# Feed-forward in four groups of inner tiles, with all but three or four tile pairs by Strassen's algorithm

## The chip, the cores and the metric

The kernel runs on one core of one Trainium2 chip. Times are device microseconds of one execution. The trace is that of one profiled execution; its engines are TensorE (PE, with its weight loads as PEld), VectorE (DVE), ScalarE (ACT), GpSimd (POOL) and SyncE (SP), which issues the DMAs.

## The reference

The program is a trunk of two layers on 512 tokens of 1024 features, all in float32. Each layer has a feed-forward, a mixer and a second feed-forward:

```python
for layer in range(DEPTH):
    x = x + 0.5 * swiglu(rmsnorm(x, ffa_norm[layer]), ffa_gate[layer], ffa_up[layer], ffa_down[layer])
    ...                                  # the mixers, which the change leaves alone
    x = x + mix
    x = x + 0.5 * swiglu(rmsnorm(x, ffb_norm[layer]), ffb_gate[layer], ffb_up[layer], ffb_down[layer])
return rmsnorm(x, final_norm)

def swiglu(x, wg, wu, wd):
    return (jax.nn.silu(x @ wg) * (x @ wu)) @ wd
```

The inner width is 2816, so a feed-forward has three products of 512 x 1024 x 2816.

## The kernel before

**Layout.** Features lie on the 128 partitions and tokens along the free dimension: `x` is 8 tiles of 128 x 512. The inner width is 22 tiles of 128 (`NF`), worked on in two halves of 11 (`HF`).

**A split product.** Each float32 operand is kept as two fp32r parts, high and low, and a product is three matmuls, high x high, high x low and low x high (`mm3`, lines 246 to 248). The two parts of a weight are made on the core: a DMA brings a raw piece of 128 x up to 1024 (`wraw`, three buffers), ScalarE copies it to the high part (line 274) and VectorE subtracts to get the low one (line 275; three buffers of each).

**A plain pair** ("S" in `PLAN`) is one inner tile of gate and up: 2 x 8 contraction tiles x 3 matmuls of 512 columns. VectorE then multiplies both with the row scale `rstd`, ScalarE takes Silu of the gate, VectorE multiplies the two and the result is split again (`hhi`, `hlo`; 11 buffers each).

**A Strassen pair** ("W", `hidden7`) does the same tile as a 2 x 2 block product: gate and up, two halves of the tokens, even and odd contraction tiles. It is 7 products of 4 contraction tiles x 3 matmuls of 256 columns (line 490). VectorE first makes the four weight sums (lines 467 and 468) and their low parts (line 474), ScalarE the high ones (line 473); afterwards ScalarE and VectorE join the results (lines 495 to 508). The sums on the side of `x` are the **column forms** (`column_forms`, lines 440 to 450): for each pair of contraction tiles four sums of 128 x 256 and their two parts, kept in the four `xi` buffers for the whole feed-forward. They are made right before the first Strassen pair. Their two inputs are scaled copies of `x` in the pool `t`, which has three buffers and serves the squares and the root mean square as well.

**The down projection** follows each half: for each pair of output tiles, 11 inner tiles x 2 x 3 matmuls of 512 columns, then VectorE adds half of the result to `x` (line 415). In the second half `set_x` makes the high and low part of the new `x`, its squares and their sum; after the last tile `set_rstd` sums them over the partitions with a matmul of ones (line 320), takes Sqrt on ScalarE and a reciprocal on VectorE (line 324).

**Order.** Every engine runs its instructions in the order that a scheduler wrote when the program was built; the program's own order sets the priorities. All raw pieces come by SP's queue, in order.

Of the kernel before, what the change touches and what calls it, by code (L numbers as in the profile page):

```python
# [12 lines left out]
AF = mybir.ActivationFunctionType  # L13
ALU = mybir.AluOpType
AX = mybir.AxisListType

P = 128
T = 512
NT = T // P
D = 1024  # L20
KD = D // P
DFF = 2816
NF = DFF // P
HF = NF // 2
# [89 lines left out]
          ("head", 2), ("val", 3), ("head", 3), ("outc", 0), ("outm", 0)]  # L114
OUT_LAST = ORDER1[-1][0]

PLAN = ("SSWSWSWWSWS", "SWSWWSWSWWS")
SCALE_DVE = ((1, 1), (3, 1))


class Trunk:
# [194 lines left out]
    def set_rstd(self, place=-70):  # L316
        nc = self.nc
        p = self.psum("aux")
        with self.tc.high_priority(place):
            nc.tensor.matmul(p, self.ones, self.acc, start=True, stop=True)  # L320
        s = self.temp()
        self.act(s, p, AF.Sqrt, bias=self.eps, scale=1.0 / D)
        self.rstd = self.cp.tile([P, T], F32, name="rstd")
        nc.vector.reciprocal(self.rstd, s)

    def load_x(self, norm, first=()):

# [39 lines left out]

    def ffn(self, wg, wu, wd, norm, load=None, out=None):
        nc = self.nc
        norm_in, self.forms = load or self.norm_in, None  # L370
        with self.phase("ffn", TURNS if load is None else TURNS[:-1]):
            if load is not None:
                self.load_x(load, (wg, wu))
            for half in range(2):
                hs = []
                for i in range(HF):
                    ft = half * HF + i
                    if PLAN[half][i] == "W":
                        if self.forms is None:
                            self.forms = self.column_forms(norm_in)  # L380
                        hs.append(self.hidden7(wg, wu, ft))
                        continue
                    ws = [self.ready.pop(0) if self.ready else self.column_weights(w, ft * P) for w in (wg, wu)]
                    pg, pu = self.psum(), self.psum()
                    cut = KD - 1 if ft == 0 else KD
                    for k0, k1 in ((0, cut), (cut, KD)):
                        for p, w in zip((pg, pu), ws):
                            for k in range(k0, k1):
                                self.mm3(p, (w[0][:, k], w[1][:, k]), self.xw[k], k == 0, k == KD - 1)
                    if self.rstd is None:  # L390
                        self.after_load()
                    g = self.tile("g")
                    nc.vector.tensor_mul(g, pg, self.rstd)
                    self.act(g, g, AF.Silu)
                    u = self.tile("u")
                    nc.vector.tensor_mul(u, pu, self.rstd)
                    nc.vector.tensor_mul(u, u, g)
                    hs.append(self.split_hidden(u))
                for dp in range(0, KD, 2):
                    if out is not None and half and dp == KD - 2:  # L400
                        self.last_down(wd, dp, hs, out)
                        continue
                    pd = [self.psum(), self.psum()]
                    for i0 in range(0, HF, 4):
                        n = min(4, HF - i0)
                        r0 = (half * HF + i0) * P
                        w = self.weights([(0, wd[r0:r0 + n * P, dp * P:dp * P + 256].rearrange(
                            "(k p) c -> p k c", p=P))], (n, 256))
                        for j, p in enumerate(pd):
                            for i in range(n):  # L410
                                self.mm3(p, (w[0][:, i, j * P:j * P + P], w[1][:, i, j * P:j * P + P]), hs[i0 + i],
                                         i0 + i == 0, i0 + i == HF - 1)
                    for j, p in enumerate(pd):
                        x = self.x[dp + j]
                        nc.vector.scalar_tensor_tensor(x, p, 0.5, x, op0=ALU.mult, op1=ALU.add)
                        if half:
                            self.set_x(dp + j, x, norm)
                            if out is not None:
                                self.finish_part(dp + j, range(NT))

    def split_hidden(self, u):
        hi, lo = self.tile("hhi", dt=FR), self.tile("hlo", dt=FR)
# [92 lines left out]
    def last_down(self, wd, dp, hs, out):  # L515

        nc = self.nc
        ws = []
        for i0 in range(0, HF, 4):
            n = min(4, HF - i0)  # L520
            r0 = (HF + i0) * P
            ws.append(self.weights([(0, wd[r0:r0 + n * P, dp * P:dp * P + 256].rearrange("(k p) c -> p k c", p=P))], (n, 256)))
        for th in range(2):
            cols, tiles = slice(256 * th, 256 * th + 256), range(2 * th, 2 * th + 2)
            pd = [self.psum()[:, :256] for _ in range(2)]
            for i in range(HF):
                w, h = ws[i // 4], [t[:, cols] for t in hs[i]]
                for j, p in enumerate(pd):
                    self.mm3(p, (w[0][:, i % 4, j * P:j * P + P], w[1][:, i % 4, j * P:j * P + P]), h, i == 0, i == HF - 1)
            for j, p in enumerate(pd):  # L530
                x = self.x[dp + j][:, cols]
                nc.vector.scalar_tensor_tensor(x, p, 0.5, x, op0=ALU.mult, op1=ALU.add)
                sq = self.temp()[:, :256]
                nc.scalar.activation(sq, x, AF.Square)
                nc.vector.tensor_add(self.acc[:, cols], self.acc[:, cols], sq)
                self.finish_part(dp + j, tiles)
            self.finish(out, tiles)
# [929 lines left out]
```

## Time and profile before

| | us |
|---|---|
| runs shown, median of 3 | 2189.73 (2188.24 to 2191.12) |
| the profiled execution, its own time | 2189.41 |
| its span, from the first to the last instruction | 2187.6 |
| TensorE busy | 2142.3 (98%) |
| VectorE busy | 1470.8 (67%) |
| ScalarE busy | 988.4 (45%) |

Matmuls are pipelined, so the durations of single ones overlap; the distance from start to start is what counts. The four feed-forwards are about 14.8 to 382.6, 776.5 to 1135.3, 1135.3 to 1495.3 and 1815.5 to 2178.2 us of the span; the mixers lie between.

### The profile page before, as it was taken

Reading aid. Unit: us, or ns where it says so; the run is one execution under the profiler, and the core shown is the slowest. Engines: PE = TensorE matmul, PEld = TensorE weight load, DVE = VectorE, ACT = ScalarE, POOL = GpSimd, SP = SyncE. Lnnn points to the kernel's source line nnn. Section 1 sums busy time; section 2 is a strip of 40 time slices with the busy share of each in tenths; the row PEclk is TensorE's granted clock in tenths of the full one; section 3 lists DMA queues with packets and bytes.
Section 4 is the critical chain, followed back from the end, with each engine's and each line's share of the span. In section 5 each row is a group of like instructions: output and inputs, shape, how many; then the busy total and the mean of one; then the engine's idle time right before and its main releaser. Section 6 shows DMA issues by size and latency. Waiting matters only on the chain.

```text
span 2187.6 us, 32169 instructions
## 1 busy us (share of the span) xinstructions
PE 2142.3 (98%) x12942; PEld 1766.3 (81%) x12942; DVE 1470.8 (67%) x2418; ACT 988.4 (45%) x1689; POOL 69.5 (3%) x70
## 2 busy tenths in 40 slices
PE   7999999999999999999999999999999999999998
PEld 5888998776667679889888989987777767988987
DVE  6854764787778788457549737745787767945753
ACT  6532443534434465234436424433368845523433
POOL 1000001000000020000010000001000001000000
PEclk9999999999999999999999999999999999999999
DMA  4433333311111034233333333326421122323331
GB/s 121 116 95 98 103 95 113 94 49 52 42 51 38 30 87 116 89 111 100 94 90 87 114 92 104 103 90 158 116 63 34 31 63 73 111 93 110 97 99 66
DMA packets 304805, 190.74 MB, mean 87 GB/s; under 512 B 19446, under 2 KB 299792, under 8 KB 304656
## 3 DMA queue, kind: packets, MB, share of 16 engines
q1 hardware_dynamic: 303536, 187.58, 29.5%
q8 instruction: 101, 1.65, 0.3%
q0 software_dynamic: 1120, 1.11, 0.3%
q14 instruction: 48, 0.39, 0.1%
HBM read 181.32 MB, written 2.10 MB: 84 GB/s over the span
## 4 chain that ended last, share of the span: by engine, by line
PE 92%; DVE 5%; ACT 1%; DMA 1%; issue 1%; POOL 0%; SPq 0%; ACTq 0%; DVEq 0%; POOLq 0%
PE ps L246 20%; PE ps L247 20%; PE ps L248 20%; PE ps L490 19%; PE ps L826 1%; PE ps L1356 1%; PE ps L808 1%; PE ps L1353 1%; DVE wlo L275 1%; DVE xi L450 1%; PE ps L1159 1%; PE ps L1337 1%; PE ps L1206 1%; PE ps L1012 0%; PE ps L929 0%
## 5 line engine op out<-in xcount | busy, mean ns | idle before, releaser
L275 DVE TENSOR_TENSOR wlo<-wraw,whi 128x1024 fp32r<-128x1024 f32 (+2 forms) x337 | 383.2, 1138 | 297.5 <-ACT whi L274 296.6
L274 ACT ACTIVATE whi<-wraw 128x1024 fp32r<-128x1024 f32 (+2 forms) x337 | 329.5, 981 | 561.8 <-PE ps L247 429.3
L246 PE MATMUL ps<-xhi,whi 128*128 128x512 f32 x1096 | 441.3, 403 | 1.0 <-ACT x L345 0.7
L247 PE MATMUL ps<-xlo,whi 128*128 128x512 f32 x1096 | 440.4, 402 | 0.4 <-DVE xlo L293 0.4
L248 PE MATMUL ps<-xhi,wlo 128*128 128x512 f32 x1096 | 439.5, 401 | 0.6
L247 PE MATMUL ps<-hlo,whi 128*128 128x512 f32 (+1 forms) x726 | 278.1, 383 | 0.0
L248 PE MATMUL ps<-hhi,wlo 128*128 128x512 f32 (+1 forms) x726 | 278.0, 383 | 0.0
L246 PE MATMUL ps<-hhi,whi 128*128 128x512 f32 (+1 forms) x726 | 277.8, 383 | 0.0
L247 PEld LDWEIGHTS ps<-xlo,whi 128*128 128x128 f32 x1096 | 208.5, 190 | 46.6 <-issue 6.1
L246 PEld LDWEIGHTS ps<-xhi,whi 128*128 128x128 f32 x1096 | 208.7, 190 | 46.1 <-issue 2.9
L248 PEld LDWEIGHTS ps<-xhi,wlo 128*128 128x128 f32 x1096 | 208.2, 190 | 45.3 <-DVE wlo L275 2.7
L490 PE MATMUL ps<-xi,shi 128*128 128x256 f32 x1056 | 193.9, 283 | 1.7 <-ACT shi L473 1.7
L490 PEld LDWEIGHTS ps<-xi,shi 128*128 128x128 f32 x1056 | 164.3, 192 | 2.6 <-ACT shi L473 1.9
L246 PEld LDWEIGHTS ps<-hhi,whi 128*128 128x128 f32 x726 | 136.5, 188 | 26.7
L247 PEld LDWEIGHTS ps<-hlo,whi 128*128 128x128 f32 x726 | 136.5, 188 | 26.5
L248 PEld LDWEIGHTS ps<-hhi,wlo 128*128 128x128 f32 x726 | 136.4, 188 | 26.4
L490 PE MATMUL ps<-xi,slo 128*128 128x256 f32 x528 | 148.4, 283 | 0.4 <-DVE slo L474 0.4
L474 DVE TENSOR_TENSOR slo<-sum,shi 128x1024 fp32r<-128x1024 f32 x88 | 107.5, 1221 | 24.0 <-ACT shi L473 24.0
L473 ACT ACTIVATE shi<-sum 128x1024 fp32r<-128x1024 f32 x88 | 93.1, 1059 | 63.5 <-DVE sum L468 30.2
L314 POOL TENSOR_TENSOR t<-t 128x512 f32<-128x512 f32 x35 | 53.0, 1514 | 1641.0 <-ACT t L310 1254.4
L490 PEld LDWEIGHTS ps<-xi,slo 128*128 128x128 f32 x528 | 100.8, 192 | 1.2 <-DVE slo L474 0.8
L490 PE MATMUL ps<-xhi,wlo 128*128 128x256 f32 x352 | 99.6, 283 | 0.0
(421 smaller groups left out, 3551.6 us busy)
## 6 DMA issues: line engine op xcount, KB each, us to landing
wraw<-in_ffa_gate_dram SPq DMA_DIRECT2D x44, 512.0 KB, 3.8
wraw<-in_ffa_up_dram SPq DMA_DIRECT2D x44, 512.0 KB, 3.8
wraw<-in_ffb_gate_dram SPq DMA_DIRECT2D x44, 512.0 KB, 3.8
wraw<-in_ffb_up_dram SPq DMA_DIRECT2D x44, 512.0 KB, 3.9
wraw<-in_ffa_down_dram SPq DMA_DIRECT2D x32, 512.0 KB, 3.4
wraw<-in_ffb_down_dram SPq DMA_DIRECT2D x32, 512.0 KB, 3.4
wraw<-in_ab_w_in_dram SPq DMA_DIRECT2D x26, 512.0 KB, 3.9
wraw<-in_cd_w_in_dram SPq DMA_DIRECT2D x18, 512.0 KB, 3.9
```

What stands on the lines that cost most here:

```text
L246: mm(out, w[0], x[0], start=start, stop=False)
L247: mm(out, w[0], x[1], start=False, stop=False)
L248: mm(out, w[1], x[0], start=False, stop=stop)
L274: nc.scalar.activation(h, raw, AF.Copy)
L275: nc.vector.tensor_sub(l, raw, h.bitcast(F32))
L314: (nc.gpsimd if self.norm_next and self.rstd is not None else nc.vector).tensor_add(self.acc, self.acc, sq)
L450: nc.vector.tensor_sub(lo, t, hi.bitcast(F32))
L473: nc.scalar.activation(hi, t, AF.Copy)
L474: nc.vector.tensor_sub(lo, t, hi.bitcast(F32))
L490: nc.tensor.matmul(out, a[:, j], b, start=first and i + j == 0, stop=i + j == 5, skip_group_check=True)
L808: mm(p[:, c * P:(c + 1) * P], BK[h, 4 * q + c, :], AR[h, 4 * q + c, :], start=True, stop=True)
L826: mm(p[h, c * LC:(c + 1) * LC], lhs[h, c, :], rhs[h, c, :], start=True, stop=True)
```

## The change

The inner tiles are taken in four groups of 5, 6, 5 and 6 instead of two halves of 11. After each pair of a group, one down part of the group before is done, as long as there is one (four parts: two output tiles each, with that group's tiles only); the last group's four parts come at the end. Only the first 4 pairs of the first feed-forward and the first 3 of the others are plain. The column forms are made behind the matmuls of the plain pair 2 (first feed-forward) or 0 (the others). The root mean square is taken as exp(-0.5 ln(mean + eps)) on ScalarE. `last_down`, the last part of the last feed-forward, takes 6 inner tiles instead of 11. Weight pieces of the down projection have up to 3 inner tiles instead of 4.

```diff
-PLAN = ("SSWSWSWWSWS", "SWSWWSWSWWS")
+PLAN = (("SSSSW", "WWWWWW", "WWWWW", "WWWWWW"), ("SSSWW", "WWWWWW", "WWWWW", "WWWWWW"))
...
-        self.act(s, p, AF.Sqrt, bias=self.eps, scale=1.0 / D)
+        self.log_exp_table()
+        self.act(s, p, AF.Ln, bias=self.eps, scale=1.0 / D)
         self.rstd = self.cp.tile([P, T], F32, name="rstd")
-        nc.vector.reciprocal(self.rstd, s)
+        self.act(self.rstd, s, AF.Exp, scale=-0.5)
...
+            below, ft = [], 0
+            for group in plan:
                 hs = []
+                for i, form in enumerate(group):
+                    hs.append((ft, self.hidden7(wg, wu, ft) if form == "W" else self.hidden8(wg, wu, ft, norm_in, plan)))
+                    ft += 1
+                    if below:
+                        self.down(wd, *below.pop(0))
+                below = [(dp, hs) for dp in range(0, KD, 2)]
+            for dp, hs in below:
+                if out is not None and dp == KD - 2:
+                    self.last_down(wd, dp, hs, out)
+                    continue
+                self.down(wd, dp, hs)
+                for k in (dp, dp + 1):
+                    self.set_x(k, self.x[k], norm)
+                    if out is not None:
+                        self.finish_part(k, range(NT))
+
+    def hidden8(self, wg, wu, ft, norm, plan):
...
+        if self.rstd is None:
+            self.after_load()
+        if ft == plan[0].index("W") - 3 + (plan is PLAN[0]):
+            self.forms = self.column_forms(norm)
+        g = self.tile("g")
+        nc.vector.tensor_mul(g, pg, self.rstd)
...
+    def down_weights(self, wd, dp, hs):
+
+        parts = [hs[i:i + 3] for i in range(0, len(hs), 3)]
+        return [(*self.weights([(0, wd[part[0][0] * P:(part[-1][0] + 1) * P, dp * P:dp * P + 256].rearrange(
+            "(k p) c -> p k c", p=P))], (len(part), 256)), [h for _, h in part]) for part in parts]
+
+    def down_products(self, out, j, part, cols, first, last):
+        hi, lo, hs = part
+        for i, h in enumerate(hs):
+            self.mm3(out, (hi[:, i, j * P:j * P + P], lo[:, i, j * P:j * P + P]), [t[:, cols] for t in h],
+                     first and i == 0, last and i == len(hs) - 1)
+
+    def down(self, wd, dp, hs):
+        pd = [self.psum(), self.psum()]
+        parts = self.down_weights(wd, dp, hs)
+        for part in parts:
+            for j, p in enumerate(pd):
+                self.down_products(p, j, part, slice(0, T), part is parts[0], part is parts[-1])
+        for j, p in enumerate(pd):
+            x = self.x[dp + j]
+            self.nc.vector.scalar_tensor_tensor(x, p, 0.5, x, op0=ALU.mult, op1=ALU.add)
```

## Rows read from the trace of the kernel before

**Rows 1.** The page's busy time of each engine, with share and instructions.

```profile
PE 2142.3 (98%) x12942; PEld 1766.3 (81%) x12942; DVE 1470.8 (67%) x2418; ACT 988.4 (45%) x1689; POOL 69.5 (3%) x70
```

**Rows 2.** The chain that ended last, by engine and by line.

```profile
PE 92%; DVE 5%; ACT 1%; DMA 1%; issue 1%; POOL 0%; SPq 0%; ACTq 0%; DVEq 0%; POOLq 0%
PE ps L246 20%; PE ps L247 20%; PE ps L248 20%; PE ps L490 19%; PE ps L826 1%; PE ps L1356 1%; PE ps L808 1%; PE ps L1353 1%; DVE wlo L275 1%; DVE xi L450 1%; PE ps L1159 1%; PE ps L1337 1%; PE ps L1206 1%; PE ps L1012 0%; PE ps L929 0%
```

**Rows 3.** Windows: one Strassen pair, one plain, two Strassen, one half's down projection.

```profile
core 0: us, PE busy (x) PEld busy (x) DVE busy (x) ACT busy (x) POOL busy (x), PEclk, DMA share, GB/s
971.41:981.48 10.07, 10.07 (x86) 10.07 (x84) 8.11 (x11) 6.07 (x9) 0.00 (x0) 1.00 0.36 104
981.48:992.39 10.91, 10.91 (x51) 9.02 (x49) 9.66 (x16) 3.48 (x5) 0.00 (x0) 1.00 0.28 82
992.39:1012.54 20.15, 20.15 (x170) 20.15 (x168) 16.42 (x24) 12.23 (x19) 0.00 (x0) 1.00 0.39 114
900.69:960.53 59.84, 59.84 (x266) 49.55 (x264) 21.77 (x25) 12.51 (x13) 0.00 (x0) 1.00 0.30 91
```

**Rows 4.** Windows: two Strassen and two plain pairs from each feed-forward's first Strassen pair.

```profile
38.98:93.23 54.25, 46.02 (x265) 40.46 (x264) 51.73 (x81) 31.92 (x44) 0.00 (x0) 0.91 0.34 98
799.98:848.65 48.67, 45.69 (x266) 40.24 (x264) 43.54 (x66) 26.44 (x38) 0.00 (x0) 0.93 0.36 98
1158.03:1205.94 47.91, 44.54 (x266) 39.14 (x264) 43.21 (x66) 26.65 (x38) 0.00 (x0) 0.96 0.35 99
1838.23:1886.63 48.40, 45.42 (x266) 40.12 (x265) 43.43 (x66) 26.39 (x39) 0.00 (x0) 0.93 0.36 99
```

**Rows 5.** Timeline of TensorE in the second feed-forward's first Strassen pair: start, length.

```profile
803.45 0.40 PE L247 MATMUL ps<-xlo,whi 128*128 128x512 f32 x1
805.69 0.39 PE L490 MATMUL ps<-xi,whi 128*128 128x256 f32 x1 [1.85 <-ACT xi L449]
...
808.80 0.63 PE L246 MATMUL ps<-xhi,whi 128*128 128x512 f32 x1
809.23 0.63 PE L247 MATMUL ps<-xlo,whi 128*128 128x512 f32 x1
```

**Rows 6.** Timeline of VectorE, five instructions in a row with no idle time.

```profile
1014.14 0.41 DVE L508 TENSOR_TENSOR u<-u,ps 128x256 f32<-128x256 f32 x1
1014.47 0.69 DVE L509 TENSOR_TENSOR g<-g,rstd 128x512 f32<-128x512 f32 x1
1015.07 0.68 DVE L511 SCALAR_TENSOR_TENSOR u<-u,rstd 128x512 f32<-128x512 f32 x1
1015.67 1.22 DVE L474 TENSOR_TENSOR slo<-sum,shi 128x1024 fp32r<-128x1024 f32 x1
1016.81 0.69 DVE L512 TENSOR_TENSOR u<-u,g 128x512 f32<-128x512 f32 x1
```

**Rows 7.** Timeline of the second feed-forward's root mean square and column forms.

```profile
788.19 1.02 PE L320 MATMUL ps<-t,c_main 128*128 128x512 f32 x2
788.57 2.36 DVE L275 TENSOR_TENSOR wlo<-wraw,whi 128x1024 fp32r<-128x1024 f32 x2 [4.36 <-ACT whi L274]
...
790.80 0.69 ACT L182 ACTIVATE t<-ps,eps 128x512 f32<-128x512 f32 x1
791.38 1.32 ACT L440 ACTIVATE t<-x,vecs_mix 128x512 f32<-128x512 f32 x2
791.52 3.35 DVE L324 RECIPROCAL rstd<-t 128x512 f32<-128x512 f32 x1 [0.59 <-ACT t L182]
...
812.36 1.23 DVE L450 TENSOR_TENSOR xi<-sum,xi 128x1024 fp32r<-128x1024 f32 x1 [0.52 <-ACT xi L449]
```

**Rows 8.** Timeline: a Strassen pair's last matmul and the end of its hidden tile.

```profile
1064.46 0.28 PE L490 MATMUL ps<-xi,slo 128*128 128x256 f32 x1
...
1068.09 0.69 DVE L424 TENSOR_TENSOR hlo<-u,hhi 128x512 fp32r<-128x512 f32 x1 [0.70 <-ACT hhi L423]
```

**Rows 9.** The page's DMA issues: KB of one, median us to landing.

```profile
wraw<-in_ffb_gate_dram SPq DMA_DIRECT2D x44, 512.0 KB, 3.8
```

More of the change, by code (lines that the diff above doesn't have):

```diff
@@ L369, in ffn @@
         nc = self.nc
-        norm_in, self.forms = load or self.norm_in, None
+        norm_in, plan = load or self.norm_in, PLAN[load is None]
         with self.phase("ffn", TURNS if load is None else TURNS[:-1]):
@@ L373, in ffn @@
                 self.load_x(load, (wg, wu))
-            for half in range(2):
+            below, ft = [], 0
+            for group in plan:
                 hs = []
[L376 to L419, printed above, removed]
@@ new lines, in hidden8 @@
+    def hidden8(self, wg, wu, ft, norm, plan):
+        nc = self.nc
+        ws = [self.ready.pop(0) if self.ready else self.column_weights(w, ft * P) for w in (wg, wu)]
+        pg, pu = self.psum(), self.psum()
+        cut = KD - 1 if ft == 0 else KD
+        for k0, k1 in ((0, cut), (cut, KD)):
+            for p, w in zip((pg, pu), ws):
+                for k in range(k0, k1):
+                    self.mm3(p, (w[0][:, k], w[1][:, k]), self.xw[k], k == 0, k == KD - 1)
+        if self.rstd is None:
[4 more added lines that the diff above has]
+        nc.vector.tensor_mul(g, pg, self.rstd)
+        self.act(g, g, AF.Silu)
+        u = self.tile("u")
+        nc.vector.tensor_mul(u, pu, self.rstd)
+        nc.vector.tensor_mul(u, u, g)
+        return self.split_hidden(u)
@@ L517, in last_down @@
         nc = self.nc
[L518 to L522, printed above, removed]
+        parts = self.down_weights(wd, dp, hs)
         for th in range(2):
@@ L525, in last_down @@
             pd = [self.psum()[:, :256] for _ in range(2)]
-            for i in range(HF):
-                w, h = ws[i // 4], [t[:, cols] for t in hs[i]]
+            for part in parts:
                 for j, p in enumerate(pd):
-                    self.mm3(p, (w[0][:, i % 4, j * P:j * P + P], w[1][:, i % 4, j * P:j * P + P]), h, i == 0, i == HF - 1)
+                    self.down_products(p, j, part, cols, part is parts[0], part is parts[-1])
             for j, p in enumerate(pd):
```

## The prediction

> **What bounds the kernel now.** I read the page first: TensorE is busy for 98% of the span, VectorE for 67% [rows 1], and the chain that ended last is TensorE's for 92%, with the three matmuls of a split product at 20% each and the line of Strassen's products at 19% [rows 2]. So a microsecond taken from TensorE's stream in a feed-forward is one taken from the end, as long as the other engines keep it fed. Next I read the windows of single pieces of one feed-forward [rows 3]: a Strassen pair is 10.07 us for 84 matmuls of 256 columns (0.1199 us each), a plain pair 10.91 us for 48 of 512 columns (0.2273 each), a half's down projection 59.84 us for 264 (0.2267 each). In all three TensorE has no gap and the clock is full. Last I read the four places where a feed-forward makes its first Strassen pair [rows 4]: each window holds two pairs of either kind, so 2 x 10.07 + 2 x 10.91 = 41.96 us of matmuls, and takes 54.25, 48.67, 47.91 and 48.40 us. There TensorE's mean clock is 0.91 to 0.96. The timeline shows why [rows 5]: TensorE waits for the column forms (lines 449 and 450), and after the wait a 512-column matmul starts every 0.43 us instead of every 0.227, that is at 1.2 GHz in place of 2.4.
>
> **The change, part by part.**
>
> *Pairs.* Before, 44 of 88 pairs are Strassen's. After, the first feed-forward keeps 4 plain ones and the others 3: 13 plain, 75 Strassen. 31 pairs go from 10.91 to 10.07 us: 31 x 0.84 = 26.0 us less. The interval is a little more than half for half the columns, so each matmul has a fixed part and the saving is 7.7% of a pair, not an eighth. The Trainium skill ("TensorE: Matmul & The Clock Gate", Back-to-back issue gap) gives N / 2.4 GHz + 2.5 ns, by which a pair would save 1.19 us and the sum would be 36.9 us. The rows do not agree with so small a fixed part, and the rows decide.
>
> *Column forms.* They move from just before the first Strassen pair to behind the matmuls of pair 0 (pair 2 in the first feed-forward), and there are now three (four) plain pairs ahead of the first Strassen pair instead of two. Today the four windows lose 199.23 - 4 x 41.96 = 31.4 us [rows 4]. If the forms are there in time all of that comes back. They cannot start much sooner than now: they need two of the three buffers of the pool t, of which the sum of squares holds one until the ones matmul at 788.19, and today they start at 791.38 and the last is written at 812.36 [rows 7]. But the need moves: the third product, the first that reads a form, starts 2.9 us (24 matmuls) into a pair that begins about 11 us later, near 814.
>
> *Root mean square.* Sqrt and a VectorE reciprocal of 3.35 us [rows 7] become Ln and Exp on ScalarE, each about the 0.69 us of the Sqrt row. It frees 3.3 us of VectorE, six times, and the scale is ready some 2.7 us sooner. TensorE works on other pairs or projections meanwhile, so I count 0 (bounds: 0, and 5 x 2.7 = 13 us if every start hung on it). One table load stays one table load.
>
> *Down parts.* The products are the same 528 x 512 columns a feed-forward. A part is 6 matmuls a tile: 6.80 us for 5 tiles, 8.16 for 6. Added are 16 additions into x a feed-forward (VectorE, 0.60 us each by the starts in [rows 6]) and 8 weight pieces with their DMA, copy and subtraction. They run under TensorE; without that cover they would cost 16 x 0.60 + 8 x about 0.6 = 14 us a feed-forward. Traffic: a pair and a part of 5 tiles bring 1.70 MB in 16.9 us, 101 GB/s, under the 114 GB/s of the stretch with two Strassen pairs [rows 3]; a piece lands in 3.8 us [rows 9]. SP issues pieces in order into three buffers, so a late VectorE subtraction delays the next piece; nothing else stands behind it. In the last part the half-width matmuls fall from 132 to 72: 0.4 us less.
>
> *VectorE's load.* By starts, an instruction of 256 columns holds it 0.33 us, of 512 0.60, of 1024 1.14 [rows 6]. A Strassen pair has four of the first, nine of the second and three of the third: 1.32 + 5.40 + 3.42 = 10.15 us, as much as its 10.07 on TensorE. A plain pair is 2 x 1.14 + 4 x 0.60 = 4.68, a part of 5 tiles about 0.85 + 0.60 + 2 x 0.60 = 2.65 (768 columns put between 512 and 1024). So in the second group VectorE has 6 x 10.15 + 4 x 2.65 = 71.5 us for TensorE's 6 x 10.07 + 4 x 6.80 = 87.6: 82%. Only a run of Strassen pairs with no part between them has no slack. There are four such runs a feed-forward, of two or three pairs. The stretch of two today shows no gap on TensorE [rows 3].
>
> *New stalls.* (a) From 788.6 until a first form is needed near 814 VectorE must do the weights of two plain pairs (2.36 + 2.28), four forms (each 4 x 0.33 + 1.14 = 2.46, in all 9.8), two plain pairs' ends (4 x 1.2 = 4.8) and of the Strassen pair one weight, two sums and one split (1.14 + 1.2 + 1.14): 22.7 of 25.4 us, and the two Strassen pairs behind it give nothing back. I put 2.5 us of stall there in three feed-forwards, 1 in the first, which has a plain pair more. (b) At the third run of three: 0.5 each. (c) The last group's first part needs the last hidden tile after 4.08 + 6 x 0.227 = 5.4 us; that tile is ready 4.2 us after a pair's last matmul when VectorE has nothing else [rows 8]: 0. (d) 0.5 a feed-forward for transitions that no row shows. Together 3 x 2.5 + 1 + 2 + 2 = 12.5 us. The lower bound is 0; the upper is the second rival's 45.
>
> *Sum.* The profiled execution took 2189.4 us (span 2187.6 and 1.8 around it), the median of the runs shown is 2189.7: no difference that matters. 2189.4 - 26.0 - 31.4 - 0.4 + 12.5 = **2144 us**. Without new stalls it is 2131.6.
>
> **Rivals.**
>
> *The forms are no earlier.* They wait for the same buffers as before, and behind the weights of three pairs; if the stall only moves with the pair, 31.4 us are not won: 2131.6 + 31.4 + 4 = 2167. For it: they start where they start today. Against: 11 us more room and 3.3 us less VectorE work. 10%.
>
> *VectorE binds in the runs.* Over two Strassen pairs today it is idle for 20.15 - 16.42 = 3.73 us [rows 3]. If this is waiting inside a pair that can't be filled, a pair needs 10.15 + 1.87 = 12.02 us, 1.95 more than TensorE, whenever a Strassen pair follows another directly: 23 times in the kernel. 2131.6 + 45 = 2176. Against: the same run of two shows no gap now. 14%.
>
> *Slower: the clock falls at each run.* If TensorE waits at the head of a run long enough to go back to 1.2 GHz, as at 803.45 [rows 5], each such event costs what that window lost, 48.67 - 41.96 = 6.7 us. The gain of 57.8 is used up from the ninth of the 16 runs; at all 16 it is 2131.6 + 107 = 2239. Against: no run without forms does it today. 6%.
>
> *Half-width matmuls cost half.* If in long Strassen stretches 256 columns took 0.1137 us, half of 0.2273, the 31 pairs would win 84 x 0.0062 = 0.52 us more each, 16 us: 2128. Every Strassen stretch shows 0.1199. 2%. The page named above leans that way: by its figures the time would be 2133.
>
> **How the numbers follow.** My forecast has 66%, with 2132 to 2156 as its own range (new stalls from 0 to 24 us). The first rival has 10, the second 14, the slower one 6, half-width 2, and 2 is left for a sum that comes out at nothing. The range goes from 2130 to 2174: the first rival and most of the second lie inside, what lies outside is under 2 in 10. About 0.2%, 4.4 us, is what a measurement of this kernel can tell from no change. Faster by more than that is 66 + 10 + 14 + 2 = 92%, within it 2%, slower 6%.
>
> **What would show it.** A run of two Strassen pairs at 20.15 us and a part of 5 tiles at 6.8 show the first and the fourth step right. No start gap over 1 us on TensorE between the first plain pair and the second group, at clock 1.00, shows the forms early; a gap that ends on line 449 or 450 shows the first rival. VectorE over 90% in the second group, with gaps on TensorE that end on a split's subtraction (line 474 before), shows the second; intervals of 0.43 us after them the slower one. The reciprocal's row must be gone. I would be wrong by most if the order that the scheduler writes for VectorE puts a pair's end ahead of the next pair's sums, since the runs have no slack to absorb it.

## The result and the profile after

| | us | ratio to the kernel before, 95% interval |
|---|---|---|
| before, in the same job | 2189.14 | |
| after, median of 4 | 2136.42 (2130.63 to 2139.65) | 0.9755 [0.9731, 0.9779] |
| after, again in two later jobs | 2140.29, 2135.64 | 0.9775 [0.9754, 0.9796], 0.9760 [0.9746, 0.9774] |
| forecast | 2144 (2130 to 2174) | |

The kernel is 52.7 us faster (2189.14 - 2136.42) where 45.4 were forecast. The profiled execution, at 2130.63 us, is the fastest of its four. Executions of one kernel in one job lie up to 10 us apart. The profiles show one part of that: stretches in the mixers in which TensorE runs at 1.2 GHz, none in this profile of the kernel after, 3.4 us in a later one of it, 6.8 us in the one before, and up to 13.7 us in the variants below. So what the change did is read inside the feed-forwards.

The page after, busy time by engine and the chain that ended last, against [rows 1, 2]:

```profile
PE 2099.0 (99%) x14028; PEld 1787.2 (84%) x14028; DVE 1667.9 (78%) x2818; ACT 1085.5 (51%) x1911; POOL 68.3 (3%) x70
PE 92%; DVE 4%; DMA 2%; ACT 1%; issue 1%; POOL 0%; SPq 0%; DVEq 0%; ACTq 0%; POOLq 0%
```

TensorE is still the bound. VectorE has 197 us more to do and hides it.

The windows after that answer to [rows 3], with the same columns: a Strassen pair, two in a row, a down part of five tiles, one of six.

```profile
828.78:838.85 10.07, 10.07 (x86) 10.07 (x84) 6.42 (x11) 4.02 (x8) 0.00 (x0) 1.00 0.49 147
972.80:992.96 20.16, 20.16 (x170) 20.15 (x169) 16.50 (x25) 11.05 (x18) 0.00 (x0) 1.00 0.31 98
821.95:828.78 6.83, 6.83 (x33) 5.64 (x31) 6.83 (x12) 3.69 (x5) 0.00 (x0) 1.00 0.21 64
964.62:972.80 8.18, 8.18 (x38) 6.76 (x37) 8.00 (x14) 2.96 (x4) 0.00 (x0) 1.00 0.28 82
```

The matmuls cost what they cost before. The windows after from the first Strassen pair of each feed-forward to the end of its first run, against [rows 4] (two pairs in the first line; in the others three, with 22 plain matmuls among them):

```profile
58.59:78.74 20.15, 20.15 (x169) 20.15 (x168) 18.91 (x29) 12.66 (x20) 0.00 (x0) 1.00 0.37 110
786.64:821.95 35.31, 35.31 (x275) 34.40 (x274) 33.77 (x52) 19.65 (x32) 0.00 (x0) 1.00 0.39 114
1131.87:1167.20 35.33, 35.33 (x276) 34.41 (x275) 33.77 (x52) 19.79 (x32) 0.00 (x0) 1.00 0.42 118
1797.68:1833.02 35.34, 35.34 (x275) 34.41 (x274) 33.81 (x52) 19.79 (x32) 0.00 (x0) 1.00 0.41 117
```

Three pairs and 22 plain matmuls are 3 x 10.07 + 22 x 0.2273 = 35.21 us, and they take 35.31 to 35.34: no stall, the clock at 1.00. All 31.4 us of [rows 4] came back. VectorE is busy for 94 to 96% of these stretches. Not all of the 31.4 us was waiting: by the mean clocks of [rows 4], 0.09 x 54.25 + 0.07 x 48.67 + 0.04 x 47.91 + 0.07 x 48.40 = 13.6 us of them, as an estimate and at most, were TensorE at 1.2 GHz. That part went with the waits.

The timeline after of the second feed-forward's root mean square and forms, against [rows 7]:

```profile
768.96 1.02 PE L321 MATMUL ps<-t,c_main 128*128 128x512 f32 x2
770.16 0.67 ACT L183 ACTIVATE t<-ps,eps 128x512 f32<-128x512 f32 x1
770.73 0.71 ACT L457 ACTIVATE t<-x,vecs_mix 128x512 f32<-128x512 f32 x1
771.35 0.62 ACT L183 ACTIVATE rstd<-t 128x512 f32<-128x512 f32 x1
...
784.05 1.22 DVE L467 TENSOR_TENSOR xi<-sum,xi 128x1024 fp32r<-128x1024 f32 x1
...
785.79 1.22 DVE L276 TENSOR_TENSOR wlo<-wraw,whi 128x1024 fp32r<-128x1024 f32 x1
...
787.11 0.45 PE L249 MATMUL ps<-xhi,wlo 128*128 128x512 f32 x1
...
793.01 1.22 DVE L491 TENSOR_TENSOR slo<-sum,shi 128x1024 fp32r<-128x1024 f32 x1
...
794.59 0.40 PE L507 MATMUL ps<-xi,shi 128*128 128x256 f32 x2
794.83 0.28 PE L507 MATMUL ps<-xi,slo 128*128 128x256 f32 x1
```

The reciprocal of 3.35 us is gone. The last form is written 16.3 us after the ones matmul (785.27 - 768.96), where it took 25.4 before, and is 9 us ahead of the first matmul that reads one (794.59). But the low part of the third plain pair's weights is written at 787.01 and read at 787.11, and the first low part of the weight sums is written at 794.23 and read at 794.83: these have 0.1 and 0.6 us to spare. VectorE, not the forms, is what this stretch is close to; the experiments bear on that.

The one stall left is at the run of three pairs between the second and the third group: 0.79, 0.13, 0.48 and 1.09 us in the four feed-forwards. The timeline after of the last of them, all engines:

```profile
1897.82 12.01 SPq L263 DMA_DIRECT2D wraw<-in_ffb_down_dram  x2
...
1908.71 0.68 DVE L485 TENSOR_TENSOR sum<-sum,wraw 128x512 f32<-128x512 f32 x1
...
1910.06 0.37 SPq L263 DMA_DIRECT2D wraw<-in_ffb_gate_dram  x1
1912.03 0.37 SPq L478 DMA_DIRECT2D wraw<-in_ffb_up_dram  x1
...
1916.60 0.69 DVE L484 TENSOR_TENSOR sum<-wraw 128x512 f32<-128x512 f32 x1 [1.14 <-DMA wraw<-in_ffb_up_dram]
...
1917.20 0.68 DVE L529 TENSOR_TENSOR u<-u,g 128x512 f32<-128x512 f32 x1
...
1917.92 0.63 ACT L440 ACTIVATE hhi<-u 128x512 fp32r<-128x512 f32 x1 [3.19 <-DVE u L529]
...
1918.46 0.37 ACT L516 ACTIVATE u<-ps 128x256 f32<-128x256 f32 x1
...
1918.88 0.39 PE L507 MATMUL ps<-xhi,shi 128*128 128x256 f32 x1 [0.79 <-ACT u L516]
```

Read it from the end. TensorE waits for ScalarE to copy a finished product out of its buffer. ScalarE has that copy behind `hhi` of the pair before, which waits for a product on VectorE. VectorE has that product behind a weight sum, which waits for the up piece. SP asked for that piece only at 1912.03, behind two down pieces and a gate piece. VectorE itself waits in this chain: the late thing is a transfer. But it was asked for late because of VectorE. SP's longest wait from 1880 to 1925 us:

```profile
SPq L263 <- DVE sum L485: 11.2, 1, 11.2
```

The second of the two down pieces waited for a raw buffer until VectorE had done the last weight sum of the pair before, at 1909.39 (1908.71 + 0.68).

### The profile page after: what moved, and what is told of

Read it like the earlier page. It is cut to its first block, busy times and chain, and to the rows that moved or that the text cites. A ratio compares the mean times of both kernels' runs of the same rounds, so it can differ in the third digit from the quotient of the medians.

```text
span 2128.9 us, 35206 instructions
## 1 busy us (share of the span) xinstructions
PE 2099.0 (99%) x14028; PEld 1787.2 (84%) x14028; DVE 1667.9 (78%) x2818; ACT 1085.5 (51%) x1911; POOL 68.3 (3%) x70
## 4 chain that ended last, share of the span: by engine, by line
PE 92%; DVE 4%; DMA 2%; ACT 1%; issue 1%; POOL 0%; SPq 0%; DVEq 0%; ACTq 0%; POOLq 0%
PE ps L507 33%; PE ps L247 15%; PE ps L248 15%; PE ps L249 15%; PE ps L838 2%; DMA wraw<-in_ffa_up_dram 1%; PE ps L1368 1%; PE ps L820 1%; PE ps L1365 1%; DVE wlo L276 1%; PE ps L1171 1%; PE ps L1218 1%; PE ps L1349 1%; PE ps L1024 1%; PE ps L941 0%
## 5 line engine op out<-in xcount | busy, mean ns | idle before, releaser
L507 PE MATMUL ps<-xi,shi 128*128 128x256 f32 x1800 | 330.4, 283 | 0.0
L507 PEld LDWEIGHTS ps<-xi,shi 128*128 128x128 f32 x1800 | 280.6, 192 | 0.0
L507 PE MATMUL ps<-xi,slo 128*128 128x256 f32 x900 | 254.5, 283 | 0.0
L247 PE MATMUL ps<-xhi,whi 128*128 128x512 f32 x600 | 244.8, 409 | 2.8 <-ACT x L347 2.6
L248 PE MATMUL ps<-xlo,whi 128*128 128x512 f32 x600 | 242.8, 405 | 0.4 <-DVE xlo L294 0.4
L249 PE MATMUL ps<-xhi,wlo 128*128 128x512 f32 x600 | 242.6, 404 | 0.0
L507 PE MATMUL ps<-xlo,whi 128*128 128x256 f32 x600 | 169.7, 283 | 0.0
L507 PE MATMUL ps<-xhi,whi 128*128 128x256 f32 x600 | 169.4, 283 | 0.0
L484 DVE TENSOR_TENSOR sum<-wraw 128x512 f32<-128x512 f32 x150 | 98.8, 686 | 81.6 <-DMA wraw<-in_ffa_up_dram 41.5
L247 PEld LDWEIGHTS ps<-xhi,whi 128*128 128x128 f32 x600 | 113.1, 188 | 30.1 <-issue 3.8
```

What stands on the lines that cost most here:

```text
L247: mm(out, w[0], x[0], start=start, stop=False)
L248: mm(out, w[0], x[1], start=False, stop=False)
L249: mm(out, w[1], x[0], start=False, stop=stop)
L484: nc.vector.tensor_add(t[:, 0], *first)
L507: nc.tensor.matmul(out, a[:, j], b, start=first and i + j == 0, stop=i + j == 5, skip_group_check=True)
```

## The experiments

Each run is set against the kernel before on the same chip (its median 2190.40, 2188.78 and 2189.29 us in the three jobs). Stalls are TensorE's start-to-start intervals over the nominal 0.1199 and 0.2273 us, summed over a place.

| run | us | ratio | stalls at the four first Strassen pairs, us |
|---|---|---|---|
| forms_late | 2140.39 | 0.9772 [0.9751, 0.9793] | none |
| forms_early_only | 2204.73 | 1.0068 [1.0049, 1.0086] | 13.6, 10.6, 10.6, 11.6 |
| two_halves; two_halves_b | 2132.26; 2132.05 | 0.9739 [0.9720, 0.9758]; 0.9742 [0.9729, 0.9756] | none |
| three_ahead | 2177.86 | 0.9948 [0.9933, 0.9963] | 9.0, 4.2, 3.1, 4.7 |
| ln_exp_before | 2187.13 | 0.9989 [0.9980, 0.9998] | 10.0, 5.7, 6.6, 5.7 |
| sqrt | 2155.07 | 0.9850 [0.9833, 0.9866] | 8.5, 2.9, 2.9, 2.9 |
| two_ahead | 2159.14 | 0.9861 [0.9847, 0.9876] | 6.0, 6.2, 6.5, 6.5 |
| pairs44 | 2158.23 | 0.9856 [0.9841, 0.9871] | none |
| no_run3 | 2131.75 | 0.9745 [0.9731, 0.9758] | none |

**The changed kernel again**, the measure for the first job.

> The changed kernel once more, for its spread. If the 4 to 9 us by which its other executions lie above the profiled one (2130.6) come from one place, a second profile may show it. Theory 1: the long place is the run of three Strassen pairs between the second and the third group, where the profiled execution lost 0.13 to 1.09 us in each feed-forward; a slower execution shows a gap of several us there and a lower clock behind it. Rival: the gaps lie at the start of the program, where the first weights and x arrive. Expected: 2130 to 2140 us.

2140.29 us, and the same profile: stalls of 0.92, 0.89, 0.63 and 1.87 us at the run of three between the second and the third group, none at the forms and none of several us. The span is 5.3 us longer (2134.2 against 2128.9). 2.5 us of that lie ahead of the first ones matmul, where the rival put them, and 2.2 in the feed-forwards.

**Where the forms stand in the program.** In the changed kernel they go back to just before the first Strassen pair:

```diff
+                    if form == "W" and ft == plan[0].index("W"):
+                        self.forms = self.column_forms(norm_in)
...
-        if ft == plan[0].index("W") - 3 + (plan is PLAN[0]):
-            self.forms = self.column_forms(norm)
```

> The changed kernel with the column forms made right before the first Strassen pair again; everything else stays, the three or four plain pairs ahead of it too. Theory 1 (where the program makes the forms decides, since it sets their place in VectorE's and ScalarE's order): most of the 31 us come back, 2136 + 20 to 30 = 2156 to 2167. Rival (the room of a plain pair more and the missing reciprocal are what hides them): within 4 us of the changed kernel, 2132 to 2141.

2140.39 us against 2140.29: no difference in the medians (this profile has 2.3 us of stalls more in the first feed-forward, at a later Strassen pair). And in the kernel before they are moved up, behind the matmuls of the first pair, and nothing else is changed:

```diff
-                        if self.forms is None:
-                            self.forms = self.column_forms(norm_in)
...
+                    if ft == 0:
+                        self.forms = self.column_forms(norm_in)
```

> The kernel before with one edit: the column forms are made behind the matmuls of pair 0 instead of right before the first Strassen pair. 44 Strassen pairs, two plain pairs ahead of the first one, Sqrt and reciprocal as before. Theory 1 (the place alone): 2189 - 31 = 2158, at least below 2170. Rival (the forms can't start sooner, since their buffers come free only with the ones matmul, so without the plain pair more most of the stall stays): 2178 to 2189.

2204.73 us, slower than before, which neither theory allowed. The forms are done 20.3 us after the ones matmul instead of 25.4, and the stall grows to 10.6 us or more. The trace of this run, TensorE's longest wait there and the VectorE rows in front of it:

```profile
812.98 0.68 DVE L275 TENSOR_TENSOR wlo<-wraw,whi 128x512 fp32r<-128x512 f32 x1
...
813.72 0.58 PE L490 MATMUL ps<-xi,wlo 128*128 128x256 f32 x1 [5.82 <-DVE wlo L275]
```

TensorE now waits for the Strassen pair's own weights, which VectorE does behind the forms. So the move of the forms, which the prediction named first there, brings nothing in the one kernel and costs 14 us in the other. What was waited for was not the forms as such.

**The third plain pair, alone in the kernel before.**

```diff
-PLAN = ("SSWSWSWWSWS", "SWSWWSWSWWS")
+PLAN = ("SSSWWSWWSWS", "SWSWWSWSWWS")
```

> The kernel before with one edit: in the first half of each feed-forward the plain pairs are moved to the front, so that three instead of two stand ahead of the first Strassen pair; 44 Strassen pairs as before, forms right before the first of them, Sqrt and reciprocal as before. Theory 1 (the room of the third plain pair is what hides the forms): 18 to 31 of the 31 us are won, 2159 to 2172. Rival (the reciprocal's 3.35 us of VectorE, in the way of the forms, is what counts): 2180 to 2190.

10.9 us less, between the two ranges given ahead; 21 us of stalls stay.

**The logarithm and exponential, alone in the kernel before**, by the diff's lines in `set_rstd`:

> The kernel before with nothing changed but the root mean square's tail: logarithm and exponential on ScalarE in place of square root there and reciprocal on VectorE; two plain pairs ahead of the first Strassen pair, column forms where they were. Theory: the 31 us of stalls at the first Strassen pairs go only with both, the third plain pair and the reciprocal's removal; this one alone brings the forms 3 to 4 us earlier in each feed-forward, so that some 17 to 25 us of the stalls stay and the time is 2173 to 2183, ratio 0.992 to 0.997. Rival: the reciprocal alone is what held the forms (the rows of TensorE's clock fall only because of it); then the stalls fall below 10 us and the time is about 2165.

2.2 us less, and 28 us of stalls stay: outside the bounds given ahead, on the other side than the rival. The last form is written 21.4 us after the ones matmul (808.68 - 787.27) instead of 25.4, but TensorE's stream resumes after 20.3 instead of 20.6 us (807.57 and 808.80, the start of the stream in [rows 5]). The waits of TensorE in that stretch of this run: what it waited for, us in total, times, longest.

```profile
PE ps L491 <- ACT xi L450: 2.5, 1, 2.5
PE ps L491 <- ACT shi L474: 0.6, 1, 0.6
PE ps L491 <- DVE xi L451: 0.3, 1, 0.3
```

What VectorE does just before the last form (its sum in line 449 is the last that ScalarE's `xi` waits for):

```profile
804.45 0.69 DVE L468 TENSOR_TENSOR sum<-wraw 128x512 f32<-128x512 f32 x1
805.05 0.42 DVE L449 SCALAR_TENSOR_TENSOR sum<-sum,t 128x256 f32<-128x256 f32 x1
805.39 0.69 DVE L469 TENSOR_TENSOR sum<-sum,wraw 128x512 f32<-128x512 f32 x1
```

A weight sum of the Strassen pair (line 468) stands ahead of it; in the kernel before, VectorE has none done when the stream resumes. Part of the time that the reciprocal gave back went into work that TensorE needs later.

**The reverse: Sqrt and reciprocal in the changed kernel.**

```diff
-        self.log_exp_table()
-        self.act(s, p, AF.Ln, bias=self.eps, scale=1.0 / D)
+        self.act(s, p, AF.Sqrt, bias=self.eps, scale=1.0 / D)
...
-        self.act(self.rstd, s, AF.Exp, scale=-0.5)
+        nc.vector.reciprocal(self.rstd, s)
```

> The changed kernel with Sqrt and the reciprocal on VectorE again. Theory 1 (the room): in the changed kernel the last form is ready about 5 us before it is read, so 3.35 us more of VectorE still fit; within 3 us of the changed kernel, 2135 to 2143. Rival (the reciprocal): three feed-forwards stall by 4 to 8 us each, 2150 to 2164.

2155.07 us: 15 to 19 us more than the three medians of the changed kernel. The first wait in the second feed-forward is for the low part of a plain pair's weights, none is for a form:

```profile
PE ps L249 <- DVE wlo L276: 1.4, 1, 1.4
```

The edit does more than put 3.35 us back on VectorE. It also puts ScalarE's load of a function table back between the ones matmul (777.99) and the scale, and VectorE idles before the reciprocal. Two rows of this run:

```profile
779.30 1.28 ACT L183 ACT_TABLE_LOAD   x1
...
781.32 3.35 DVE L325 RECIPROCAL rstd<-t 128x512 f32<-128x512 f32 x1 [0.59 <-ACT t L183]
```

In the changed kernel the load for the logarithm and exponential stands ahead of the ones matmul (768.96):

```profile
740.10 1.28 ACT L190 ACT_TABLE_LOAD   x1
```

No run separates the reciprocal from the load. In the first feed-forward the idle time is 2.22 us and the stall 8.5; in the others 0.59 and 2.9.

**One plain pair less in the changed kernel** (79 Strassen pairs, so 4 x 0.84 = 3.4 us fewer matmuls; the forms are put behind the first pair that allows it):

```diff
-PLAN = (("SSSSW", "WWWWWW", "WWWWW", "WWWWWW"), ("SSSWW", "WWWWWW", "WWWWW", "WWWWWW"))
+PLAN = (("SSSWW", "WWWWWW", "WWWWW", "WWWWWW"), ("SSWWW", "WWWWWW", "WWWWW", "WWWWWW"))
```

> The changed kernel with one plain pair less at the front (three in the first feed-forward, two in the others), 79 Strassen pairs, the forms behind pair 1 or 0. The four converted pairs save 4 x 0.84 = 3.4 us. Theory 1 (the room): the forms are done 16 us after the ones matmul and are now read 15 us after it, and the pair's own sums come behind them, so 2 to 7 us of stall in three feed-forwards and some in the first: 2141 to 2162. Rival (the reciprocal, or the place, hides them, not the room): 2132 to 2139.

2159.14 us, 19 to 24 us more than the changed kernel, with 25.2 us of stalls.

These four kernels and the changed one have one thing in common. The windows from about the ones matmul to the end of a main wait in the second feed-forward (in the changed kernel, which has none, to the Strassen pairs' long stretch), the fourth number of each being VectorE's busy time: three_ahead, ln_exp_before, sqrt, two_ahead, and after.

```profile
785.00:813.16 28.16, 25.99 (x128) 21.75 (x126) 27.48 (x42) 21.43 (x28) 0.00 (x0) 1.00 0.20 56
```

```profile
787.65:807.57 19.92, 16.64 (x87) 13.59 (x85) 19.38 (x35) 17.09 (x24) 0.00 (x0) 1.00 0.09 27
```

```profile
778.50:798.30 19.80, 18.36 (x82) 14.64 (x80) 19.12 (x30) 17.07 (x22) 0.00 (x0) 1.00 0.19 54
```

```profile
775.50:795.00 19.50, 15.44 (x80) 12.80 (x78) 19.48 (x35) 16.56 (x24) 0.00 (x0) 1.00 0.10 28
```

```profile
769.30:792.20 22.90, 22.90 (x103) 18.73 (x101) 22.86 (x38) 18.42 (x26) 0.00 (x0) 1.00 0.24 69
```

The kernel before has it too:

```profile
788.57:808.80 20.23, 17.25 (x84) 14.02 (x83) 19.55 (x29) 16.18 (x22) 0.00 (x0) 0.95 0.09 27
```

In all of them VectorE is busy for 97 to 100% of the time, while what TensorE waits for differs from kernel to kernel: a form, `shi`, `wlo`. I read from this that the stretch is VectorE's; no run takes work off VectorE there and leaves all else as it is. Its queue holds the forms, the plain pairs' weights and ends, and the Strassen pair's sums, in one order; a stall comes at whichever of them TensorE reaches first. In the changed kernel the same 100% are just enough.

**The number of Strassen pairs alone.** The changed kernel with 44 of them, as before, the groups and all else kept:

```diff
+PLAN = (("SSSSW", "SWSWSW", "SWSWW", "SWSWWW"), ("SSSWW", "SWSWSW", "SWSWS", "SWSWWW"))
```

> The changed kernel with 44 Strassen pairs instead of 75, spread over the later groups; three or four plain pairs at the front, four groups and early forms stay. Theory 1 (31 pairs at 0.84 us each are the first term of the sum): 2138 + 26 = 2164, 2160 to 2168. Rival (Strassen pairs in long runs lose part of it to waits): 10 to 20 us more than the changed kernel, 2148 to 2158.

2158.23 us, between the two ranges given ahead and 18 to 23 us above the three medians of the changed kernel. By the traces, from the ones matmul to the last down product, the feed-forwards take 4.8, 12.1 (second and third together) and 5.3 us more than in the profiled execution of the changed kernel, 22.2 in all. That one has 2.5 us of stalls at the run of three between the second and the third group and this one, which has no such run, none, so 31 pairs bring 24.7 us of the 26.0 counted.

**No interleaving at all.** The same 75 Strassen pairs in two halves of 11 tiles, with each half's down projection behind it and pieces of four tiles as before:

```diff
+PLAN = (("SSSSWWWWWWW", "WWWWWWWWWWW"), ("SSSWWWWWWWW", "WWWWWWWWWWW"))
...
-                    if below:
-                        self.down(wd, *below.pop(0))
...
+                if group is plan[0]:
+                    while below:
+                        self.down(wd, *below.pop(0))
```

> The changed kernel with its 75 Strassen pairs and early forms, but in two halves of 11, each followed by its down parts, so 7 or 8 and then 11 Strassen pairs stand in a row. Theory 1 (VectorE's 10.15 us a pair are as much as TensorE's 10.07 and it needs some waiting on top; the down parts between the pairs are what pays for it): 0.5 to 1.95 us lost for each pair in a row, about 70 of them, so 35 to 137 us more: 2171 to 2273. Rival (TensorE stays fed in long runs, as in the runs of two, and the four groups bring nothing): 2130 to 2142.

2132.26 us beside 2140.29 for the changed kernel in the same job, as the rival had it; timed again beside it:

> The same kernel as two_halves (two halves of 11 tiles, 75 Strassen pairs in runs of 7 or 8 and of 11, no down part between pairs), timed again beside the changed kernel to settle which is faster. Theory now: a run of Strassen pairs needs no down part between its pairs, and the four groups cost what they add, the stalls behind late up pieces at the third run of three (2.5 to 4.3 us in the feed-forwards measured so far). Expected 2 to 5 us below the changed kernel in this job, 2132 to 2138. Rival: the 8 us between the two medians of the first job were the executions' own scatter (half-clock stretches in the mixers, 0 to 14 us), and the two come out within 1.5 us of each other.

> The changed kernel once more, the measure for two_halves_b and no_run3. Both theories: 2134 to 2142, ratio 0.975 to 0.978 to the kernel before; three or four stalls of 0.3 to 2 us ahead of a Strassen pair's products at the run of three pairs between the second and the third group, none elsewhere in the feed-forwards.

2132.05 beside 2135.64 us. The window of the longest run of that second profile, 11 Strassen pairs:

```profile
933.63:1044.50 110.87, 110.87 (x925) 110.86 (x924) 106.31 (x164) 66.47 (x107) 0.00 (x0) 1.00 0.36 102
```

924 matmuls in 110.87 us are 0.1200 each, without a gap, and VectorE is busy for 96%. The mean hides where it is idle; the first pair of the run, and the nine behind it:

```profile
933.63:943.70 10.07, 10.07 (x85) 10.06 (x84) 6.61 (x9) 5.12 (x8) 0.00 (x0) 1.00 0.41 116
943.70:1034.41 90.71, 90.71 (x758) 90.71 (x757) 89.93 (x143) 55.92 (x90) 0.00 (x0) 1.00 0.34 94
```

From the second pair on VectorE is busy for 99%, 9.99 us a pair, and TensorE has no gap. The Strassen pairs need no down parts between them.

**No run of three between the second and the third group.** A group of six leaves out the down part after its third and sixth pair, not after its fifth and sixth:

```diff
-                    if below:
+                    if below and not (len(group) == 6 and i in (2, 5)):
```

> The changed kernel, where a group of six pairs leaves out the down part after its third and its sixth pair and not after its fifth and sixth, so that no run of three Strassen pairs stands between the second and the third group. Theory: the stall there comes of the two down parts in front of the run, whose pieces of weights are asked for ahead of the next pair's on one queue, so that its up piece lands late; with runs of two alone the stalls of 0.3 to 1.9 us fall to under 0.3 us each and the time is 2 to 4 us below again_b. Rival: it is VectorE's load at that place (the run of three itself), then the first run of three, at the end of the first group and the begin of the second, would stall as well, which it did not; or the down pieces press on the queue wherever they stand, then stalls of the same size turn up behind other down parts and the time is the same within 1.5 us.

2131.75 beside 2135.64 us, and the stalls are gone. The run of two in the last feed-forward, window and SP's timeline in this run:

```profile
1901.29:1921.44 20.15, 20.15 (x169) 20.14 (x168) 17.92 (x28) 11.27 (x18) 0.00 (x0) 1.00 0.36 113
```

```profile
1901.15 5.14 SPq L263 DMA_DIRECT2D wraw<-in_ffb_down_dram  x2
1906.83 0.37 SPq L263 DMA_DIRECT2D wraw<-in_ffb_gate_dram  x1
1910.48 0.37 SPq L478 DMA_DIRECT2D wraw<-in_ffb_up_dram  x1
```

The two down pieces are out within 5.14 us instead of 12.01, and the up piece 9.3 us after the first of them instead of 14.2. The first run of three, and the runs of 11 with no down piece among their weights, don't stall, so a run of three by itself is not the reason. SP's wait for the weight sum falls from 11.2 us to 4.4:

```profile
SPq L263 <- DVE sum L485: 4.4, 1, 4.4
```

Both two_halves and no_run3 come out ahead of the changed kernel. In the medians it is 3.6 and 3.9 us in the last job, where the intervals of the ratios still overlap. The traces say the same with less scatter: added as above, the feed-forwards take 1344.9 and 1345.2 us in two_halves and 1344.8 in no_run3, against 1347.2, 1349.4 and 1347.5 in the three profiles of the changed kernel. That is 2 to 4.6 us, about the stalls.

## Why the prediction was right, step by step

The mechanism, its sign and its size were right; two steps were right for another reason than the one given, and the root mean square was mis-sized.

**Pairs, -26.0.** Right: -24.7. The Trainium skill ("TensorE: Matmul & The Clock Gate", Back-to-back issue gap) has N / 2.4 + 2.5 ns for a matmul by itself, by which an estimate for 256 columns is 109 ns; the run of 11 pairs measures 120 again, so the row and not the rule gave the saving.

**Column forms, -31.4.** The sum was right, the reason only in part. All of it came back. But the forms' new place does nothing, and no single edit does it: the third plain pair alone brings 10.9 us, the logarithm and exponential alone 2.2, and each taken out of the changed kernel costs 15 us or more. No run puts just these two into the kernel before; forms_late and pairs44 have both, within the four groups, and show no stall there. The need for the forms was counted right: TensorE reads the first one 25.6 us after the ones matmul (794.59 - 768.96; in the prediction 814 - 788.2). That they cannot start much sooner was wrong by 1.4 us: their first input is made 1.8 us after the ones matmul (770.73 - 768.96) where it took 3.2. VectorE is full from the ones matmul to the first Strassen products. A third plain pair gives it 10.91 us of TensorE's time for 4.68 of its own work, and the reciprocal gives back 3.35. Why the two bring 2.2 and 10.9 us alone and 31 together stays open. Two things that bear on it are shown: with each edit VectorE's order is written anew (in ln_exp_before a weight sum goes ahead of the last form), and a gap is followed by matmuls at 1.2 GHz [rows 5], so that a stall isn't proportional to what VectorE lacks.

**Root mean square, 0.** This is the term that was mis-sized. I reasoned that TensorE has other pairs while the scale is made, so that a shorter chain to the scale is worth nothing. But the reciprocal also takes 3.35 us of VectorE, in a stretch without slack. With it back, three feed-forwards stall by 2.9 us each, about that; the first stalls by 8.5, which 3.35 us don't cover. Together these are 17.2 us, and the run lost 15 to 19. The upper bound of 13 in the prediction was near, by luck: it was worked out from the chain. The chain was misread as well. "One table load stays one table load" holds for the number, not the place: before, the load stands behind the ones matmul (the sqrt run shows it at 779.30), after, ahead of it, and the scale is ready 3.7 us sooner (3.0 us after the ones matmul, before 6.7), not 2.7. What the load's place is worth no run shows. The Trainium skill ("ScalarE: Activation LUTs", What it computes) advises, in place of the Rsqrt function with its accuracy issues, VectorE's reciprocal followed by a Sqrt. In this kernel that form, in the order Sqrt and reciprocal, is slower than the exponential of a logarithm: 3.35 us on VectorE and 0.69 on ScalarE against 0.67 and 0.62 on ScalarE.

**New stalls, +12.5.** Point (a), 8.5 us where the forms meet the first Strassen pair, came out at 0. My count of 22.7 us of work in 25.4 was the right thing to look at, and the trace shows how near it was: VectorE busy for 22.86 of 22.90 us, a plain pair's `wlo` 0.1 us and `slo` 0.6 us ahead of their use. That it fits without a stall is close to luck. Point (b), 2 us at a run of three (the one between the second and the third group), measured 2.5 (4.3 in the second profile), but through a late up piece, behind a buffer that VectorE freed late, and not through a lack of slack inside the run. Points (c) and (d) are 0.

**Down parts, 0.** Nearly: 6.83 us for 6.80 and 8.18 for 8.16, for 32 parts of each size some 1.6 us. Down parts between pairs were said to give VectorE its slack; the run of 11 shows that TensorE stays fed without any. The 10.15 us of VectorE a pair were counted about right (9.99 measured); that VectorE would need slack on top was wrong. The down parts' pieces are in the way at the one stall that is left.

**Sum.** The profiled feed-forwards went from 1400.3 to 1347.2 us, 53.1 less; 26.0 + 31.4 + 0.4 - 2.5 - 1.6 gives 53.7, and 52.4 with the 24.7 measured for the pairs. The other 5.6 us by which the profiled spans differ (58.7 - 53.1) lie ahead of the first ones matmul (2.4) and in the mixers and the tail, of which the change touches only the root mean square; most of that part is the second mixer's, where the profile before has its 6.8 us at 1.2 GHz. Against the median the forecast was 7.6 us too high: 8.5 + 2 of stalls that did not come, less 0.5 + 1.6, is 8.4.

**Rivals.** The forms were earlier, by 9 us. VectorE, full as it is, does not bind in the runs; ahead of the first Strassen pair it does, as I read the windows, and a reciprocal or one plain pair less decides. The clock fell at no run of the changed kernel's profile. Half-width matmuls stayed at 0.120 us. An order of VectorE's that puts a pair's end ahead of the next pair's sums was feared; the stall that is left comes of the opposite, a sum (line 484) ahead of a pair's end (line 529).

## What to carry to other kernels

When an engine waits for a late value, look at the whole queue of the engine that makes it: if that is busy without a gap, moving the value up can make the next one late, and a microsecond taken from that queue, from whichever instruction, counts only if what is waited for comes up by it (taking the reciprocal out alone brought 2.2 us). Test edits that relieve the same queue both alone and taken out of the full set; here they brought 2 and 11 us alone and cost 15 and more when taken out. Interleaving another stage's work to give an engine slack also puts that stage's transfers into the queue; run the long stretch without it before building it in.

## What was not expected of the hardware

Nothing in the durations: 0.120 and 0.227 us a matmul, 3.35 us for the reciprocal and 0.67 and 0.62 us for the logarithm and exponential of 128 x 512 stood in every run that has them. Unexpected was how full VectorE can be without TensorE noticing: 89.93 of 90.71 us over nine pairs in a row, and 22.86 of 22.90 ahead of the first Strassen pair.
